# Layer 1 attention of a two-layer decoder trunk: scores of both tiles of tokens in one step

## The chip, the cores and the metric

The kernel runs on one core of one Trainium2 chip. The metric is the device time of one execution in microseconds (us); times below are medians of runs of the same program. The engines are named as in the profile: PE is TensorE's matmuls, PEld its weight loads, DVE is VectorE, ACT is ScalarE, POOL is GpSimd, SP the queue that issues the loads.

## What is computed

Two layers of a decoder trunk on 256 tokens of width 1024, all in float32. Layer 0 has eight heads of block-sparse attention and eight of dilated windows; layer 1 has 16 heads in four groups with three branches, added with sigmoid gates. Each layer ends with a gated feed-forward block and a gated per-layer embedding. The part of layer 1 that the change touches, cut down:

```python
q, kc, vc, ks, vs, kw, vw, g = jnp.split(xn @ w_in, ...)
kc = _rms(_compress(_heads(kc, NSA_GROUPS), *cmp_k), kn_c)     # 15 compressed keys
vc = _compress(_heads(vc, NSA_GROUPS), *cmp_v)
gates = jax.nn.sigmoid(g)                                      # per token, head, branch
s = einsum('bghsd,bgcd->bghsc', qg, kc) * ATTN_SCALE + bias    # branch 1: compressed
o_cmp = softmax(s) @ vc
# branch 2: selected blocks (with 256 tokens: all of them, causal)
# branch 3: sliding window of 512 (with 256 tokens: all, causal)
o = gates[..., 0:1] * o_cmp + gates[..., 1:2] * o_slc + gates[..., 2:3] * o_win
return o.transpose(0, 2, 1, 3).reshape(B, S, D_MODEL) @ w_out
```

## The kernel before

Activations stay on chip, with the features on the partitions. Weights come in units of up to 512 KB: SP loads a unit into one of six `raw` buffers, ACT makes its rounded high part (`hi`), DVE (in layer 1 also POOL, for half of every second unit) the low part (`lo`), and the main matmuls use both. In layer 1 the main matmuls are, in order, the projection chunks (`ic`), the projection of the per-layer embedding (`pa`), the output projection (`oc`), then the feed-forward block (`ga`, `ua`, `da`).

PSUM has eight banks: four for the main accumulators (tag `acc`) and four small ones (tag `st`, `st_tile`, line 76) that all other steps take in turn.

The order of PE and SP is written out by hand. The program keeps an estimated clock `clk`, which every matmul advances by a fixed cost, and a list `side` of generators, each with a due time. After every four to six main matmuls, `tick` (line 169) lets up to six due generators emit a step each; a generator yields the time until it wants to be asked again. `until` (line 174) runs side steps, and nothing else, until a named event has happened by the clock. Where such a step lies in PE's queue is thus fixed when the program is built. ACT, DVE and POOL get their order from the framework.

The side steps of layer 1:

- `compress` (966) makes the 15 compressed keys and values; its last step (`kct`) transposes the keys and sets the event `kc`.
- `split_t`/`q_split` (933) transposes the queries (`qps`).
- `cmp_scores(b)` (1048), once for each half of the heads: scores of the compressed branch (`cs`), a long softmax on DVE and ACT, and, `KN["cmp"]` later, the transposes of its probabilities (`pcp`).
- `attend` (699) drives, for eight heads, the steps of `attn1` (1098). `A(i)` (1102): scores (`s`) of one pair of heads for one tile of 128 tokens, both branches, six matmuls into two small banks; then on DVE four readings with the bias (`neg_scores`, 499), on ACT four exponentials, a reciprocal, and the normalising, on POOL for the first tile and on DVE for the second. The second tile's step also emits a load of the next bias tile on SP (`load_tb1`, 893, called at 1122), into the buffer of a pair whose readings must be over. `B(i)` (1131): two sets of three transposes (`t`) of one head's probabilities into two small banks, copied out by ACT and DVE. `C(k)` (1144): 18 matmuls that give a pair's output (`o`) in one small bank, read by ACT and then DVE (`o_evac`, 495).

`attend` is called with `pb=2, per_a=2, per_s=2` in layer 1: two A steps make a pair, at most two heads may be open when a pair begins, the gap between A steps is `gap1` = 2.4, and B is due `LB1` = 7.66 after the pair's last score step. Layer 0 calls it with `per_s` 1 (lines 829 and 835). `out_proj` (536) waits with `until` for the outputs of two pairs before each quarter of `oc`.

Of the kernel before, what the change touches and what calls it, by code (L numbers as in the profile page):

```python
# [11 lines left out]
F32 = mybir.dt.float32  # L12
# [20 lines left out]


OUT = (1024, 256)
KN = {'stQ': 3.5, 'stF': 7.12, 'stP': 6.0, 'st0': 1.48, 'st1': 11.0, 'sq': 3, 'LSb': 2, 'warm': 4, 'spF': 6.77, 'spP': 5.23, 'burst': 6, 'prep0': 2.6, 'prep1': 2.0, 'qk': 11.39, 'qk2': 12.0, 'qk3': 9.53, 'qk4': 10.0, 'ev': 0.63, 'gap0': 1.54, 'gap1': 2.4, 'LB0': 7.35, 'LB1': 7.66, 'LC': 2.13, 'hT': 5.0, 'cmp': 10.0, 'ev1': 1.0, 'ev2': 1.8, 'c0': 4.0, 'c00': 0.5, 'c1': 4.5, 'c2': 9.0, 'ns': 'PPVV', 'lop': 2, 'ptd': 1, 'pb': 1}


@with_exitstack
def trunk(ctx: ExitStack, tc: tile.TileContext, a, out):  # L40
# [5 lines left out]
    ps = ctx.enter_context(tc.tile_pool(name="ps", bufs=1, space=PS))  # L46
# [26 lines left out]
    def acc_tile(n):  # L73
        return ps.tile([128, 512], F32, tag="acc", name=n, bufs=4)

    def st_tile(n):
        return ps.tile([128, 512], F32, tag="st", name=n, bufs=4)

    def wk_tile(n, shape=(128, 512)):
# [42 lines left out]
    def emit_split():  # L122
# [8 lines left out]
        m = N if i < 3 else n  # L131
        if KN["lop"] and i in l1_units and i % KN["lop"] == 0:
            m = n // 2
        for x in range(0, n, m):
            nc.scalar.activation(hi[:, x:x + m], r[:, x:x + m], AF.Copy)  # L135
            e = nc.gpsimd if KN["lop"] and x and i in l1_units and i % KN["lop"] == 0 else nc.vector
            e.tensor_tensor(lo[:, x:x + m], r[:, x:x + m], hi[:, x:x + m].bitcast(F32), op=OP.subtract)  # L137
# [8 lines left out]
    clk = [0.0]  # L146
    ev = {}
# [11 lines left out]
    def side_step():  # L159
        for e in side:  # L160
            if e[1] <= clk[0]:
                try:
                    e[1] = clk[0] + next(e[0])
                except StopIteration:
                    side.remove(e)
                return True
        return False

    def tick():
        for _ in range(KN["burst"]):  # L170
            if not side_step():
                return
# [24 lines left out]
    def happened(name):  # L197
        return name in ev and ev[name] <= clk[0]

    def take(name, n):  # L200
# [3 lines left out]
        while ws["ld"] < min(i + n + LD, len(units)):  # L204
            emit_load()
        while ws["sp"] < min(i + n + (LS if n == 1 else KN["LSb"]), len(units)):
            emit_split()
# [148 lines left out]
    warm = wk_tile("warm")  # L356
# [8 lines left out]

    keep_busy(KN["warm"])
    nc.scalar.activation(rhb[:, 0:2], ones, AF.Tanh)
# [34 lines left out]
    st = {}  # L402
# [15 lines left out]
    def squares(i):  # L418
# [4 lines left out]
        else:  # L423
            j = wk_tile("sqj")
            nc.scalar.activation(j, two(h, i), AF.Square)  # L425
            e = nc.gpsimd if i < KN["sq"] else nc.vector
            e.tensor_tensor(st["sum"], st["sum"], j, op=OP.add)  # L427
# [271 lines left out]
    def attend(n, A, B, C, gap, lb, p0, ready=(), pb=3, ptb=4, per_pt=1, per_a=1, per_s=1):  # L699

        tA, tB, k, steps, tS = [], [], 0, 0, 0.0
        while 2 * k < n:
            now = clk[0]
            if len(tB) >= 2 * k + 2 and now >= tB[2 * k + 1] + KN["LC"] and all(happened(n) for n in ready):
                C(k)
                ev[f"o{p0 + k}"] = clk[0] + 0.8
                k += 1
                yield 0.0
            elif len(tB) < len(tA) and now >= tA[len(tB)] + lb and (len(tB) - 2 * k) // per_pt < ptb:
                B(len(tB))  # L710
                tB.append(clk[0])
                if len(tB) == n - 2:
                    ev[f"b{p0}"] = clk[0]
                yield 0.0
            elif len(tA) < n and (steps % 2 or len(tA) - len(tB) <= (pb - 1) * per_a) and now >= tS:
                A(steps)
                steps += 1
                tS = clk[0] + gap
                if per_s == 1 or steps % 2 == 0:
                    tS = clk[0] + gap * per_a / per_s  # L720
                    tA += [clk[0] + 0.5 * KN["gap0"] * i for i in range(per_a)]
                yield 0.0
            else:
                yield 0.15
# [241 lines left out]
    def compress(idr):  # L966
# [57 lines left out]
        kc = cmc  # L1024
# [18 lines left out]
        new_x(1)  # L1043
        cmp_homes(0)
        vc_blocks(0)
        ev["kc"] = clk[0] + 0.8

    def cmp_scores(b):
        if b:
# [48 lines left out]
    def attn1(h0):  # L1098
# [44 lines left out]

        def C(k):
            pts = [stt.pop(("pt", 2 * k + e)) for e in range(2)]
            o = ps.tile([128, 512], F32, tag="st", name="o", bufs=4)
            j, gs = k, (h0 // 4, h0 // 4 + 1)
            b = h0 // 8
            for l in range(2):
                mm(o[:, 0:256], VCR[b][:, l, 128 * (j % 2):128 * (j % 2) + 128], PCR[b][:, j // 2], start=l == 0, stop=False)  # L1150
            for br in range(2):
                for t, (x0, x1) in enumerate(((0, 256), (256, 384))):
                    for e in range(2):
                        mm(o[64 * e:64 * e + 64, 128 * t:256], VV[:, t, br, gs[e] * 64:(gs[e] + 1) * 64],
                                         pts[e][:, br, x0:x1], start=False, stop=br == 1 and t == 1)
            o_evac(o, 1, h0 // 2 + k)
# [105 lines left out]
```

## Time and profile before

| what | value |
|---|---|
| median of 3 runs | 706.35 us (705.91 to 706.37) |
| the profiled execution | 707.13 us, of which its span 705.3 us |
| PE busy | 689.8 us (98%) |
| DVE busy | 511.0 us (72%) |
| ACT busy | 413.1 us (59%) |
| POOL busy | 177.6 us (25%) |
| HBM traffic | 171 GB/s over the span |

The span reaches from the first to the last instruction of the profiled execution; its whole time has some 1.8 us around it. In the profile, a busy time of PE contains the modelled ends of matmuls that overlap the next ones, so the start of one matmul to the start of the next is the safer measure of what it cost. A row's bracket tells how long the engine was idle before it, and what ended that. The attention of layer 1 lies between 396 and 487 us.

### The profile page before, as it was taken

How to read it: one execution, taken by the hardware profiler on the slowest of the kernel's cores; microseconds unless marked ns; L12 is line 12 of the kernel's file. 1: busy time of each engine (PE TensorE's matmuls, PEld its weight loads, DVE VectorE, ACT ScalarE, POOL GpSimd, SP SyncE). 2: the span in 40 equal slices, each digit the busy share in tenths (PEclk: the TensorE clock that was granted, in tenths of full speed). 3: DMA queues.
4: the chain of work that ended last, by engine and by line, in shares of the span. 5: the costliest groups of instructions: out<-in, count | busy, mean ns of one | idle time of the engine just before them, and what ended most of it. 6: DMA issues, size and time to landing. Idle time of an engine off the chain costs nothing.

```text
span 705.3 us, 12005 instructions
## 1 busy us (share of the span) xinstructions
PE 689.8 (98%) x4378; PEld 598.0 (85%) x4378; DVE 511.0 (72%) x985; ACT 413.1 (59%) x770; POOL 177.6 (25%) x287
## 2 busy tenths in 40 slices
PE   8999999999999999999999989999999999999997
PEld 6887788998888888889878868878988888888897
DVE  6769775878867774657977788776697778757466
ACT  7547785655655653544664787776465656545343
POOL 1254100133132230001163625341232321310010
PEclk9999999999999999999999999999999999999999
DMA  8955433456566465556773355523557565654611
GB/s 305 328 181 197 164 119 120 139 183 208 165 202 200 163 225 187 183 176 194 213 238 113 118 140 126 155 61 91 153 185 228 163 198 169 218 187 170 213 60 60
DMA packets 69947, 121.66 MB, mean 172 GB/s; under 512 B 5504, under 2 KB 17664, under 8 KB 69888
## 3 DMA queue, kind: packets, MB, share of 16 engines
q1 hardware_dynamic: 69888, 120.89, 53.9%
q8 instruction: 34, 0.56, 0.3%
q14 instruction: 25, 0.20, 0.1%
HBM read 119.83 MB, written 1.05 MB: 171 GB/s over the span
## 4 chain that ended last, share of the span: by engine, by line
PE 80%; DVE 6%; ACT 4%; POOL 3%; issue 3%; DMA 3%; SPq 0%; DVEq 0%; ACTq 0%; POOLq 0%
PE ua L153 18%; PE da L153 17%; PE ga L153 17%; PE oc L153 6%; PE pc L153 5%; PE ic L153 5%; DVE lo L137 3%; PE o L153 3%; PE t L157 2%; PE s L153 2%; PE q L153 2%; PE pa L153 1%; PE v L153 1%; ACT hi L135 1%; DMA raw<-in_w_in_ab_dram 1%
## 5 line engine op out<-in xcount | busy, mean ns | idle before, releaser
L137 DVE TENSOR_TENSOR lo<-raw,hi 128x1024 fp32r<-128x1024 f32 (+2 forms) x218 | 264.2, 1224 | 104.5 <-ACT hi L135 104.4
L135 ACT ACTIVATE hi<-raw 128x1024 fp32r<-128x1024 f32 (+4 forms) x231 | 223.7, 987 | 156.5 <-PE da L153 50.7
L153 PE MATMUL ua<-x,hi 128*128 128x512 f32 (+1 forms) x384 | 96.1, 375 | 0.0
L153 PE MATMUL ga<-x,hi 128*128 128x512 f32 x352 | 92.8, 394 | 1.4 <-DVE h L521 0.9
L153 PE MATMUL da<-big,hi 128*128 128x512 f32 x352 | 89.6, 393 | 0.0
L153 PE MATMUL ic<-hi,x 128*128 128x512 f32 (+2 forms) x256 | 78.5, 376 | 0.2 <-DVE qn L924 0.2
L153 PEld LDWEIGHTS ua<-x,hi 128*128 128x128 f32 x384 | 65.9, 189 | 8.7
L153 PEld LDWEIGHTS da<-big,hi 128*128 128x128 f32 x352 | 62.7, 189 | 10.7
L153 PEld LDWEIGHTS ga<-x,hi 128*128 128x128 f32 x352 | 61.6, 189 | 11.4 <-DVE h L521 1.2
L427 POOL TENSOR_TENSOR sum<-sum,sqj 128x512 f32<-128x512 f32 x12 | 16.9, 1409 | 174.8 <-ACT sqj L425 174.7
L604 POOL TENSOR_TENSOR th<-th,rfb 128x512 f32<-128x512 f32 x22 | 28.5, 1297 | 125.1 <-DVE th L603 118.7
L153 PE MATMUL ua<-x,lo 128*128 128x256 f32 x352 | 57.6, 282 | 0.0
L153 PEld LDWEIGHTS ua<-x,lo 128*128 128x128 f32 x352 | 52.9, 190 | 5.2
L153 PEld LDWEIGHTS ga<-x,lo 128*128 128x128 f32 x352 | 51.3, 189 | 5.6
L153 PEld LDWEIGHTS ic<-hi,x 128*128 128x128 f32 x256 | 46.6, 188 | 10.3 <-issue 2.1
L153 PE MATMUL ga<-x,lo 128*128 128x256 f32 x352 | 52.8, 281 | 0.0
L153 PEld LDWEIGHTS da<-big,lo 128*128 128x128 f32 x352 | 49.1, 190 | 4.2
L153 PE MATMUL da<-big,lo 128*128 128x256 f32 x352 | 50.3, 282 | 0.0
L153 PE MATMUL oc<-x,hi 128*128 128x256 f32 x256 | 48.5, 289 | 0.1
L153 PE MATMUL ic<-lo,x 128*128 128x512 f32 (+2 forms) x128 | 46.9, 366 | 0.0
L153 PE MATMUL pc<-x,hi 128*128 128x256 f32 x256 | 46.6, 284 | 0.0
L613 POOL TENSOR_TENSOR th<-us,th 128x512 f32<-128x512 f32 x20 | 36.4, 1819 | 37.6 <-DVE us L571 37.6
(206 smaller groups left out, 1136.8 us busy)
## 6 DMA issues: line engine op xcount, KB each, us to landing
raw<-in_w_ffn_gate_dram SPq DMA_DIRECT2D x44, 512.0 KB, 3.8
raw<-in_w_ffn_up_dram SPq DMA_DIRECT2D x44, 512.0 KB, 4.4
raw<-in_w_ffn_down_dram SPq DMA_DIRECT2D x44, 512.0 KB, 4.0
raw<-in_w_in_ab_dram SPq DMA_DIRECT2D x23, 512.0 KB, 6.6
raw<-in_w_ple_gate_dram SPq DMA_DIRECT2D x16, 512.0 KB, 3.9
raw<-in_w_in_nsa_dram SPq DMA_DIRECT2D x12, 512.0 KB, 4.6
raw<-in_w_out_ab_dram SPq DMA_DIRECT2D x8, 512.0 KB, 3.3
raw<-in_w_in_nsa_dram SPq DMA_DIRECT2D x16, 256.0 KB, 4.4
```

Source lines behind the costliest of these rows:

```text
L135: nc.scalar.activation(hi[:, x:x + m], r[:, x:x + m], AF.Copy)
L137: e.tensor_tensor(lo[:, x:x + m], r[:, x:x + m], hi[:, x:x + m].bitcast(F32), op=OP.subtract)
L153: nc.tensor.matmul(o, l, r, start=start, stop=stop)
L157: nc.tensor.transpose(o, i, ident if idn is None else idn)
L427: e.tensor_tensor(st["sum"], st["sum"], j, op=OP.add)
L604: nc.gpsimd.tensor_tensor(v2(th), v2(th), r2(), op=OP.mult)
L613: nc.gpsimd.tensor_tensor(y, x, y, op=OP.mult)
```

## The change

Three things are changed. In `attend`, a layer 1 step emits the scores of both tiles of a pair (`A` twice), and only when the planner's clock is 1.2 us (`mA`) past the last time that a small bank was handed out; for 1.5 us (`mB`) after it neither of the two `attend` generators emits anything, and the next pair is due 2.6 us (`gA`) after it. For layer 0 the limit of open heads is now asked at every step, not at every second one. The event `kc` is set 1.4 instead of 0.8 after the transposes of the compressed keys, and `cmp` is 11.6 instead of 10.0. `C` takes its bank through `st_tile`, so that the clock of the last bank counts it as well.

```diff
-KN = {'stQ': 3.5, ... 'cmp': 10.0, ...}
+KN = {'mA': 1.2, 'gA': 2.6, 'mB': 1.5, 'stQ': 3.5, ... 'cmp': 11.6, ...}
...
+    used, held = [0.0], [0.0]
+
     def st_tile(n):
+        used[0] = clk[0]
         return ps.tile([128, 512], F32, tag="st", name=n, bufs=4)
...
-            if len(tB) >= 2 * k + 2 and now >= tB[2 * k + 1] + KN["LC"] and all(happened(n) for n in ready):
+            if per_s == 2 and now < held[0]:
+                yield held[0] - now
+            elif len(tB) >= 2 * k + 2 and now >= tB[2 * k + 1] + KN["LC"] and all(happened(n) for n in ready):
                 C(k)
...
-            elif len(tA) < n and (steps % 2 or len(tA) - len(tB) <= (pb - 1) * per_a) and now >= tS:
-                A(steps)
-                steps += 1
-                tS = clk[0] + gap
-                if per_s == 1 or steps % 2 == 0:
-                    tS = clk[0] + gap * per_a / per_s
-                    tA += [clk[0] + 0.5 * KN["gap0"] * i for i in range(per_a)]
+            elif len(tA) < n and len(tA) - len(tB) <= (pb - 1) * per_a and now >= tS and (
+                    per_s == 1 or now >= used[0] + KN["mA"]):
+
+                for _ in range(per_s):
+                    A(steps)
+                    steps += 1
+                if per_s == 2:
+                    held[0] = clk[0] + KN["mB"]
+                tS = clk[0] + (KN["gA"] if per_s == 2 else gap * per_a)
+                tA += [clk[0] + 0.5 * KN["gap0"] * i for i in range(per_a)]
                 yield 0.0
...
-        ev["kc"] = clk[0] + 0.8
+        ev["kc"] = clk[0] + 1.4
...
-            o = ps.tile([128, 512], F32, tag="st", name="o", bufs=4)
+            o = st_tile("o")
```

## Rows read from the trace of the kernel before

**Rows 1.** The page, its first part: busy us, share of the span, instructions.

```profile
PE 689.8 (98%) x4378; PEld 598.0 (85%) x4378; DVE 511.0 (72%) x985; ACT 413.1 (59%) x770; POOL 177.6 (25%) x287
```

**Rows 2.** By window: us, busy of PE, PEld, DVE, ACT, POOL, clock, DMA, GB/s.

```profile
396.00:441.80 45.80, 42.83 (x307) 33.79 (x305) 39.39 (x145) 35.09 (x106) 20.24 (x34) 1.00 0.45 115
441.80:487.00 45.20, 44.11 (x361) 36.54 (x360) 30.54 (x125) 31.50 (x100) 14.04 (x18) 1.00 0.36 103
```

**Rows 3.** The chain of waits: start us, us, what; undisturbed side steps.

```profile
404.35 0.90 PE s L153 x6
...
428.40 0.55 PE s L153 x6
...
435.62 1.37 PE t L157 x12
```

**Rows 4.** PE timeline, 399 to 410: start, us, operation, [idle before <- releaser].

```profile
399.97 0.40 PE L153 MATMUL ic<-hi,x 128*128 128x512 f32 x1
400.94 1.93 PE L153 MATMUL cs<-kct,big 128*128 128x64 f32 x16 [0.58 <-DVE kct L1042]
...
408.67 0.50 PE L153 MATMUL ic<-hi,x 128*128 128x512 f32 x1
409.01 0.40 PE L153 MATMUL ic<-lo,x 128*128 128x512 f32 x1
409.24 0.62 PE L153 MATMUL ic<-hi,x 128*128 128x512 f32 x2
```

**Rows 5.** PE timeline around the first transposes of the compressed probabilities.

```profile
413.78 0.39 PE L153 MATMUL ic<-hi,x 128*128 128x512 f32 x1
415.73 0.74 PE L157 MATMUL pcp<-ident,big 128*128 128x128 f32 x4 [1.56 <-ACT big L1086]
416.30 0.82 PE L157 MATMUL t<-ident,p 128*128 128x128 f32 x6
...
418.39 0.62 PE L153 MATMUL s<-big,big 64*128 64x256 f32 x6
```

**Rows 6.** PE timeline: transposes behind scores, scores behind transposes.

```profile
424.57 1.03 PE L157 MATMUL t<-ident,p 128*128 128x128 f32 x6
...
426.73 0.48 PE L153 MATMUL pa<-px,hi 128*128 128x256 f32 x2
...
445.33 0.50 PE L153 MATMUL s<-big,big 64*128 64x512 f32 x1
...
447.36 0.50 PE L153 MATMUL oc<-x,hi 128*128 128x256 f32 x2
```

**Rows 7.** PE timeline, 463 to 469.

```profile
463.78 1.07 PE L157 MATMUL t<-ident,p 128*128 128x128 f32 x6
464.78 1.32 PE L153 MATMUL s<-big,big 64*128 64x512 f32 x6
...
466.87 0.35 PE L153 MATMUL s<-big,big 64*128 64x256 f32 x1
...
468.04 0.50 PE L153 MATMUL o<-x 128*128 128x256 f32 x2
```

**Rows 8.** SP timeline (issue of a bias load), then the chain's load behind it.

```profile
407.91 0.37 SPq L897 DMA_DIRECT2D tb<-in_tb_dram  x1
...
409.10 5.22 DMA raw<-in_w_out_nsa_dram
```

**Rows 9.** DVE by line and shape, 396 to 487: busy us, mean ns | idle before.

```profile
L500 DVE CUSTOM_DVE_ANT_0 p<-s,tb 128x256 f32<-128x256 f32 x20 | 7.5, 415 | 0.5 <-PE s L153 0.4
...
L500 DVE CUSTOM_DVE_ANT_0 p<-s,tb 128x128 f32<-128x128 f32 x20 | 4.8, 280 | 0.3 <-PE s L153 0.3
```

**Rows 10.** The chain of waits around the end of the last C step.

```profile
481.75 1.71 PE o L153 x18
...
483.49 0.40 ACT x L496
...
483.90 0.44 DVE x L497
```

More of the change, by code (lines that the diff above doesn't have):

```diff
@@ L35 @@
 OUT = (1024, 256)
-KN = {'stQ': 3.5, 'stF': 7.12, 'stP': 6.0, 'st0': 1.48, 'st1': 11.0, 'sq': 3, 'LSb': 2, 'warm': 4, 'spF': 6.77, 'spP': 5.23, 'burst': 6, 'prep0': 2.6, 'prep1': 2.0, 'qk': 11.39, 'qk2': 12.0, 'qk3': 9.53, 'qk4': 10.0, 'ev': 0.63, 'gap0': 1.54, 'gap1': 2.4, 'LB0': 7.35, 'LB1': 7.66, 'LC': 2.13, 'hT': 5.0, 'cmp': 10.0, 'ev1': 1.0, 'ev2': 1.8, 'c0': 4.0, 'c00': 0.5, 'c1': 4.5, 'c2': 9.0, 'ns': 'PPVV', 'lop': 2, 'ptd': 1, 'pb': 1}
+KN = {'mA': 1.2, 'gA': 2.6, 'mB': 1.5, 'stQ': 3.5, 'stF': 7.12, 'stP': 6.0, 'st0': 1.48, 'st1': 11.0, 'sq': 3, 'LSb': 2, 'warm': 4, 'spF': 6.77, 'spP': 5.23, 'burst': 6, 'prep0': 2.6, 'prep1': 2.0, 'qk': 11.39, 'qk2': 12.0, 'qk3': 9.53, 'qk4': 10.0, 'ev': 0.63, 'gap0': 1.54, 'gap1': 2.4, 'LB0': 7.35, 'LB1': 7.66, 'LC': 2.13, 'hT': 5.0, 'cmp': 11.6, 'ev1': 1.0, 'ev2': 1.8, 'c0': 4.0, 'c00': 0.5, 'c1': 4.5, 'c2': 9.0, 'ns': 'PPVV', 'lop': 2, 'ptd': 1, 'pb': 1}
 @with_exitstack
```

## The prediction

> **What bounds the kernel now.** I read the page first, then the busy time by stretch, then the chain of waits, and last the TensorE timeline of layer 1's attention. The page says that TensorE is busy for 98% of the span [rows 1]. The stretch in which the changed steps run, 396 to 487 us, holds 42.83 + 44.11 = 86.94 us of TensorE work in 91.00 us, at a granted clock of 1.00, the 2.4 GHz level [rows 2]. So the bare idle time there is 4.06 us, and no change of order can win much more than that plus what hides inside "busy". Something does hide: a TensorE step that is held up in its middle counts as busy until its modelled end. I therefore measure from start to start. The chain gives the undisturbed lengths: scores of the first tile of tokens 0.55 us, of the second 0.90, twelve transposes 1.37 [rows 3]. Against these, six places of the timeline are too long. One row of a main matmul starts 0.24 us before the next one (409.01 to 409.24) [rows 4].
>
> - **cs** (compressed scores) starts 0.97 us after the matmul before it, not 0.24: 0.73 lost, to the compressed keys [rows 4].
> - **pcp** starts 1.95 us after its predecessor: 1.71 lost. The row names the ACT copy of the compressed probabilities [rows 5]. Behind that stands the SP queue: the bias load of pair 0 went out only at 407.91, since it waits for that pair's last score readers, and the weight load behind it took from 409.10 another 5.22 us [rows 8]. ACT, which works in order, sat on the split of those weights.
> - **The transposes behind pcp**: 416.30 to 418.39 is 2.09, 0.72 over [rows 5].
> - **Transposes straight behind scores**: 424.57 to 426.73 is 2.16, 0.79 over. I read this as banks that the scores have just filled [rows 6].
> - **Scores straight behind transposes**: 445.33 to 447.36 is 2.03, 1.13 over [rows 6].
> - **The tail**, 463.78 to 468.04: t, s, t, s take 4.26 where 1.37 + 0.90 + 0.55 = 2.82 would do, 1.44 over [rows 7].
>
> Sum: 0.73 + 1.71 + 0.72 + 0.79 + 1.13 + 1.44 = **6.52 us** of lost TensorE time that a better order could give back.
>
> **The change, part by part.**
>
> *Layer 0.* Its `attend` has `per_s` 1, so the new wait and the hold do not apply. What is new is that the odd steps must obey the limit of outstanding heads too. In the present order each of those steps comes when at most four heads are open, and four are allowed (`pb` 3, two heads a step); the due time comes out alike. No instruction moves: 0.
>
> *The order in layer 1.* I walked the side list through by hand with the planner's own costs. The first pair waits for 1.2 us after `kct`, so it comes one tick of main matmuls later than now, with both tiles, and cs comes straight behind it. Then: one pair; two B steps, a tick, the third pair; a tick, pcp, two B steps, C, and straight behind it the fourth pair. So all four pairs of the first half are scored when the last `ic` chunk ends, where now two and a half are. `q_split` of the second half is pushed at the end of that chunk, hence later in the order, and the fifth pair too; that costs nothing as long as `oc` matmuls stand in front, and they do. In the second half two pairs are scored between `oc` steps. After the fourth `oc` unit comes a run without any main matmul: B, B, pcp, pair, C, B, B, pair, C, B, B. Only then the `oc` matmuls go on.
>
> *Saved 1: the six places.* cs and pcp come later by the two due times (0.6 and 1.6), filled with main matmuls: 0.73 + 1.71. Moreover the pair's bias load goes out sooner: pair 0's second tile is scored about 3 us earlier, so its readers end earlier, and SP's weight loads behind the bias load with them. That is the cover of the pcp gain; without it the 1.71 stays. The next three bias loads are moved likewise, each behind the scores of its own pair. The other four places go as places: transposes no longer stand between the two tiles. All 6.52 are counted as removed, and the new waits are counted below.
>
> *Saved 2: fewer steps.* If the streaming time goes with the columns, the second tile (0.90) has twice the first's (0.55), so 0.35 is streaming and **0.20 us** of each step is fixed [rows 3]. Eight steps go away: 1.60. The main matmul behind a step pays as well: 0.34 to its successor, where 0.24 is usual [rows 4]; eight of these would make 0.8 more. I take 1.60, since several joined steps have no main matmul behind them; ends 0 (the pair pays the fixed part twice all the same) and 2.40.
>
> *Added 1: four banks at once.* The scores of one pair now go into all four `st` banks. A step straight ahead must have been read out, and a step straight behind waits for the first readers. VectorE needs at most 4 x 0.280 + 4 x 0.415 = 2.78 us for the eight readings [rows 9]. A C step's bank is free 0.88 us after its last matmul (481.75 + 1.71 to 483.90 + 0.44) [rows 10]; transposes ahead of scores cost the 1.13 above. The planner's rule asks for 1.2 us since the *start* of the last step, which a C step outlasts by itself, so it protects little there. Place by place:
> - first pair, whose fourth bank is that of `kct`: 0.3.
> - pairs with a tick of main matmuls behind the transposes: 0.3 in all.
> - the fourth pair straight behind C: its last bank is wanted some 0.5 us after C, free after 0.88: 0.4.
> - in the run without main matmuls, the pair behind pcp: 0.8; the pair straight behind four transposed tiles: near the 1.13, 1.0.
> - transposes behind a pcp or a C: 0.3 each, three times.
> - cs or C straight behind a pair: their bank's two readings (2 x 0.28) end while the second tile streams (0.69): 0.
> Sum 0.3 + 0.3 + 0.4 + 0.8 + 1.0 + 0.9 = **3.7 us**. The ends are 0 and the full price of both neighbours at all eight pairs, 8 x (0.79 + 1.13) = 15.4. I stay near the low end since a wait in the planner (`mB`) keeps B and C out for 1.5 us, and main matmuls fill it at five of the eight pairs.
>
> *Softmax latency.* Pair to B stays at 7.66 us in the planner, and by the walk no B step comes sooner behind its pair than 6.5 us. Eight exponentials instead of four arrive at ACT together, but in total nothing is added on VectorE, ACT or GpSimd. Counted at 0; if that cover fails, the first B of the run without main matmuls shows it.
>
> **Sum.** 6.5 + 1.6 - 3.7 = 4.4 us. The profiled execution took 707.13 us, of which 705.3 are its span; it lies 0.78 above the median of 706.35, so the gain is taken off the median: 706.35 - 4.4 = 701.95, **702.0 us**. The stages behind are bound by TensorE and keep their length, so that the gain reaches the end.
>
> **Rivals.**
>
> *Slower: the banks.* One mechanism: with all four banks in one step, TensorE waits at both neighbours of the pair at the price it pays today, 0.79 + 1.13 = 1.92 each time [rows 6]. The point from which it decides is (6.5 + 1.6) / 8 = 1.0 us a pair; above 1.2 the kernel is slower by more than 0.2%. At five of eight pairs it is 9.6 - 8.1 = 1.5 us slower, 707.9; at six 3.4, 709.8. For it: the run without main matmuls, and C straight ahead of a pair. Against it: five pairs have main matmuls on one side at least. The Trainium skill speaks for this rival: "Perfetto Trace Analysis", Optimizing Tensor Performance, says that independent matmul groups should rotate through the banks, so that reading out one overlaps the matmuls of the next; a pair that takes all four leaves nothing to rotate. By that rule the waits of [rows 6] would come at every pair; the trace agrees that they exist, and no run here shows how often they would come.
>
> *About the same: VectorE.* Up to 441.80 it is busy 39.39 of 45.80 us, 86% [rows 2]. The same work in 42 us would be 94%, and banks would come free late. If the first half can't shrink at all, the second half remains: 1.13 + 1.44 recovered, half of the fixed parts (0.8), less its own new waits (0.8 + 1.0 + 0.6): 1.0 us faster, 705.4. For it: that share. Against it: much of VectorE's work there is for weight splits, which follow the main matmuls, not the pairs.
>
> *Only the due times work.* 0.73 + 1.71 = 2.4 stay and the joined steps give back what they cost: 703.9, inside the forecast's own band.
>
> *More.* New waits of 1.5 us or less and the full fixed part: 6.5 + 1.6 - 1.5 = 6.6, 699.7.
>
> **How the numbers follow.** A kernel like this can be told from no change from about 0.2%, 1.4 us, on. Forecast with the due times alone inside its band (700.5 to 704.9): 0.53. More than that: 0.10. VectorE, within 0.2%: 0.19. Slower, the banks: 0.18. The range leaves out half of "more" and most of "slower" beyond 708.3: 699.5 to 708.3. Faster 0.53 + 0.10 = 0.63, same 0.19, slower 0.18.
>
> **What would show it.** Right: no idle before cs and pcp; eight score steps of twelve matmuls, each near 1.25 us; the start of the last `oc` unit, now behind C at some 483.4 [rows 10], near 479; the bias loads on SP at about 403, 410, 418 and 425. Wrong: score steps of 2 us or more, with ACT or VectorE readers of `t` or `o` as releasers; B steps that wait for p; VectorE above 93% of the first half; a wait of the main matmuls for weights. If cs or pcp still waits, the due times missed their cover.

## The result, and the profile after

The changed kernel takes **713.41 us** (median of 4 runs, 713.27 to 714.03); the kernel before, run beside it, 706.13 (4 runs). The ratio is 1.0099, with a 95% interval of 1.0081 to 1.0117. The prediction was 702.0 us, in a range that ended at 708.3: wrong in sign, and outside the range.

The profiled execution has a span of 711.6 us. The first part of its page (busy us, share, instructions):

```profile
PE 693.2 (97%) x4378; PEld 601.7 (85%) x4378; DVE 510.9 (72%) x985; ACT 412.8 (58%) x770; POOL 178.5 (25%) x287
```

The counts are those of [rows 1]: the same instructions in another order. By window, with the columns of [rows 2], the attention as a whole and then two stretches of it:

```profile
396.00:441.80 45.80, 42.29 (x295) 33.62 (x294) 35.94 (x136) 34.35 (x107) 20.47 (x34) 0.96 0.48 119
441.80:487.00 45.20, 41.08 (x320) 33.46 (x319) 30.88 (x128) 29.46 (x96) 13.19 (x18) 0.92 0.27 83
403.00:406.80 3.80, 3.80 (x11) 2.93 (x11) 3.13 (x13) 1.96 (x5) 2.17 (x4) 0.55 0.78 206
464.50:471.60 7.10, 6.91 (x33) 4.25 (x33) 4.35 (x26) 5.11 (x22) 3.72 (x7) 0.52 0.07 25
```

The joined step, the twelve score matmuls of two tiles, is called a pair below. Two things stand here. TensorE did fewer matmuls in the same windows (295 + 320, before 307 + 361). And the granted clock, 1.00 all along in [rows 2], fell to about half, the 1.2 GHz level, in two places. The waits of TensorE from 396 to 487 (total, times, longest), the first four:

```profile
PE pcp L160 <- DVE nm L503: 2.8, 2, 1.5
PE t L160 <- DVE big L1137: 1.2, 1, 1.2
PE s L156 <- DVE x L500: 1.0, 1, 1.0
PE t L160 <- DVE nm L503: 0.8, 1, 0.8
```

All four releasers are VectorE; the waits left out are 0.4 us and less, two of them on ACT. `nm` is the last part of a reading of scores, `big` at 1137 is the normalising, `x` at 500 the reading of `o`; the lines correspond to 500, 1129 and 497 of before.

**Where the time went.** From the start of the `kct` transposes to the first `ga` matmul the profiled executions take 92.72 us before and 99.44 after, 6.72 us more; the two spans differ by 6.3 (711.6 and 705.3), so the whole difference lies here. Summed from the start of each TensorE instruction to the start of the next, by the step it belongs to:

| step | before | after | difference |
|---|---|---|---|
| scores `s`, 96 matmuls | 13.71 | 17.53 | +3.82 |
| transposes `t`, 96 | 12.95 | 15.43 | +2.48 |
| outputs `o`, 144 | 14.51 | 16.20 | +1.69 |
| main `ic`, 54 | 15.31 | 14.57 | -0.74 |
| `cs`, `pcp`, `qps` | 5.50 | 5.07 | -0.43 |
| main `pa`, `oc`, and `kct` | 30.74 | 30.63 | -0.11 |

A wait ahead of a step is in the row of the step before it. So the waits of cs and pcp in [rows 4, 5] are in `ic` of before, and the new waits of pcp are in `s` of after.

The TensorE timeline of after in the first half (start, us, operation, [idle before <- releaser]):

```profile
399.08 1.92 PE L156 MATMUL s<-big,big 64*128 64x256 f32 x12
400.93 1.96 PE L156 MATMUL cs<-kct,big 128*128 128x64 f32 x16
402.74 0.48 PE L156 MATMUL ic<-hi,x 128*128 128x512 f32 x1
...
407.26 1.32 PE L156 MATMUL s<-big,big 64*128 64x256 f32 x12
408.50 0.50 PE L156 MATMUL ic<-hi,x 128*128 128x512 f32 x1
...
415.51 1.32 PE L156 MATMUL s<-big,big 64*128 64x256 f32 x12
418.32 0.63 PE L160 MATMUL pcp<-ident,big 128*128 128x128 f32 x4 [1.49 <-DVE nm L503]
```

The pair at 407.26 gives way to a main matmul 1.24 us later: this is the joined step as forecast. cs follows its pair without idle time. But twelve rows of `ic` behind cs take 4.52 us (402.74 to 407.26), where the same twelve take 2.94 undisturbed: the clock. And pcp, which the change moves out of a wait, waits again, for the readings of the pair straight ahead of it: 2.81 us from the start of that pair to pcp. VectorE at that place:

```profile
414.00 1.58 DVE L1093 TENSOR_TENSOR big<-csw,x 128x120 f32<-128x120 f32 x2
415.50 0.60 DVE L1137 TENSOR_SCALAR p<-p,rl 128x256 f32<-128x256 f32 x2
416.02 0.60 DVE L1137 TENSOR_SCALAR big<-big,rl 128x256 f32<-128x256 f32 x2
416.55 1.21 DVE L140 TENSOR_TENSOR lo<-raw,hi 128x1024 fp32r<-128x1024 f32 x1
417.69 0.28 DVE L503 CUSTOM_DVE_ANT_0 big<-s,tb 128x128 f32<-128x128 f32 x1
```

VectorE comes to the first reading at 417.69, 2.18 us after the pair began: the normalising of an earlier pair and a weight split stand ahead of it in the queue. The two operations ahead of these took 1.58 us, where the same two take 0.47 at 459.12; GpSimd was at work beside them (last section). In the second half, the run without main matmuls:

```profile
457.57 1.32 PE L156 MATMUL s<-big,big 64*128 64x256 f32 x12
460.23 0.63 PE L160 MATMUL pcp<-ident,big 128*128 128x128 f32 x4 [1.33 <-DVE nm L503]
...
462.18 0.77 PE L160 MATMUL t<-ident,big 128*128 128x128 f32 x5 [1.22 <-DVE big L1137]
463.75 0.52 PE L160 MATMUL t<-ident,big 128*128 128x128 f32 x3 [0.80 <-DVE nm L503]
464.44 0.58 PE L160 MATMUL t<-ident,big 128*128 128x128 f32 x3 [0.17 <-DVE rl L1133]
464.95 1.51 PE L156 MATMUL s<-big,big 64*128 64x256 f32 x7
466.65 1.62 PE L156 MATMUL s<-big,big 64*128 64x512 f32 x5 [0.19 <-DVE nm L503]
468.20 0.80 PE L156 MATMUL o<-x 128*128 128x256 f32 x2
468.92 2.81 PE L156 MATMUL o<-pt,big 128*64 128x256 f32 x16
```

TensorE was idle for 3.5 us between 458.8 and 464.5; then come scores and `o` at half clock, the sixteen matmuls of `o` with 2.81 us where 1.52 is usual. VectorE and GpSimd in the same run:

```profile
457.83 1.27 DVE L140 TENSOR_TENSOR lo<-raw,hi 128x1024 fp32r<-128x1024 f32 x1 [0.93 <-ACT hi L138]
...
459.51 0.28 DVE L503 CUSTOM_DVE_ANT_0 p<-s,tb 128x128 f32<-128x128 f32 x1
...
460.43 1.44 DVE L140 TENSOR_TENSOR lo<-raw,hi 128x512 fp32r<-128x512 f32 x1
461.79 1.13 DVE L1137 TENSOR_SCALAR big<-big,rl 128x256 f32<-128x256 f32 x4
462.84 0.41 DVE L503 CUSTOM_DVE_ANT_0 p<-s,tb 128x256 f32<-128x256 f32 x1
```

```profile
460.05 1.26 POOL L140 TENSOR_TENSOR lo<-raw,hi 128x512 fp32r<-128x512 f32 x1
```

The pair scored at 451.81 is normalised at 461.79 to 462.92, up to 9.9 us after the end of its scores (453.06); the B step behind it waited for just that. Two weight splits, and the first four readings of the next pair, stood ahead of it. Not all of that was VectorE's queue: on ACT the pair's last exponential stood behind a weight split too (456.76, 1.04 us) and began only at 457.71.

### The profile page after: what moved, and what is told of

Its sections match the earlier page's. It is cut to its first block, busy times and chain, and to the rows that moved or that the text cites. A ratio compares the mean times of both kernels' runs of the same rounds, so it can differ in the third digit from the quotient of the medians.

```text
span 711.6 us, 12002 instructions
## 1 busy us (share of the span) xinstructions
PE 693.2 (97%) x4378; PEld 601.7 (85%) x4378; DVE 510.9 (72%) x985; ACT 412.8 (58%) x770; POOL 178.5 (25%) x287
## 3 DMA queue, kind: packets, MB, share of 16 engines
HBM read 119.83 MB, written 1.05 MB: 170 GB/s over the span
## 4 chain that ended last, share of the span: by engine, by line
PE 81%; DVE 8%; ACT 4%; POOL 3%; issue 3%; DMA 2%; SPq 0%; ACTq 0%; DVEq 0%; POOLq 0%
PE ua L156 17%; PE da L156 17%; PE ga L156 17%; PE ic L156 6%; PE oc L156 5%; PE pc L156 4%; DVE lo L140 3%; PE o L156 3%; PE t L160 2%; PE v L156 2%; PE s L156 2%; PE q L156 2%; PE pa L156 1%; ACT hi L138 1%; DMA raw<-in_w_in_nsa_dram 1%
```

## The experiments

Ratios are against the kernel before, run on the same chip beside it, with 95% intervals; "0.2%" is the bound of the prediction. The first theory from these two traces was: the walk put pcp and cs in the wrong places, and the rest is the clock. The rivals were the due times, the joined step itself, the SP queue and VectorE's queue.

### Due times and places

**due_only**: the kernel before with the two due times.

```diff
-KN = {... 'cmp': 10.0, ...}
+KN = {... 'cmp': 11.6, ...}
-        ev["kc"] = clk[0] + 0.8
+        ev["kc"] = clk[0] + 1.4
```

> The kernel before with the two due times of the change alone (kc 1.4, cmp 11.6); scores as before, one tile of tokens in a step. Theory (the loss comes from the joined score steps, through waits and two falls of the granted clock): this kernel recovers the waits before cs and pcp, 0.73 + 1.71 = 2.4 us, and loses nothing: about 703.9, clock 1.00 all through. Rival (the due times do the harm, since pcp then falls behind scores): 708 or more.

Measured: 709.43 us (10 runs), 1.0034 [1.0022, 1.0046]. Slower by 0.3% instead of faster by 2.4 us. pcp still waits, and now behind transposes:

```profile
416.23 0.52 PE L157 MATMUL t<-ident,p 128*128 128x128 f32 x3 [0.77 <-DVE nm L500]
417.71 0.64 PE L157 MATMUL pcp<-ident,big 128*128 128x128 f32 x4 [0.97 <-DVE pt L1139]
```

Behind them the granted clock is 0.53 from 418.0 to 425.2. Moving a step by time does not move the work it waits for; it changes what stands ahead of it.

**due_undone**: the changed kernel with the two old due times (the same two lines turned round).

> The changed kernel with the two due times set back (kc 0.8, cmp 10.0); scores joined. Theory: the joined steps carry the loss. The first pcp no longer stands behind the third pair, which saves its 1.5 us, the run without main matmuls in the second half stays as it is, with its waits and its half clock (some 3.5 us): 711 to 713. Rival (the due times do the harm): back to about 706.

Measured: 712.69 us, 1.0080 [1.0053, 1.0108]. So most of the loss needs no due time. The first pcp's wait is gone, and waits of 1.57, 1.38 and 0.87 us stand ahead of scores instead, the middle one on ACT.

**cs_apart**: the first cs one tick later, pcp where it was.

```diff
-        yield KN["cmp"]
+        yield KN["cmp"] - (0 if b else 1.28)
...
-wait(KN["ev1"]), cmp_scores(0)
+wait(KN["ev1"] + 1.0), cmp_scores(0)
```

> The changed kernel; the first cs step comes one tick of main matmuls (six of 512 columns) later, everything else in the same place. Theory (the first fall of the clock, 403.3 to 406.7, comes from the scores of a pair with cs straight behind, 3.7 us of small matmuls): no fall there, the twelve ic matmuls behind take 2.9 instead of 4.5 us, total 711.5 to 712. Rival (the clock falls there whatever stands around): unchanged, 713.4.

Measured: 713.33 us, 1.0090 [1.0065, 1.0116]. The fall of the clock at 403 is gone. But the next pair waits 1.0 us for the reading of cs (`csw`), and the fall in the second half is longer, from 462.2 to 472.5, where the changed kernel's goes from 464.8 to 471.6. So what the first fall costs by itself is not shown by this run.

**pcp_apart**: the changed kernel with `cmp` 12.6, so that pcp stands a tick behind the pair, the order that the prediction priced.

> The changed kernel with cmp 12.6 in place of 11.6: the first pcp comes one tick behind the third pair, with B, B, C and the fourth pair behind it, which is the order that the prediction was worked out for; in the second half two B steps stand ahead of pcp. If the prediction only had the order wrong, and its prices right: 702 to 704. Theory (the prices were wrong too: in the run without main matmuls the B steps wait for the softmax and the clock falls): the 1.5 us before the first pcp go, the second half stays: 710 to 712.

Measured: 716.27 us, 1.0131 [1.0106, 1.0156], slower still. pcp waits 0.2 us, but the C step behind it finds the compressed probabilities not yet copied by ACT:

```profile
423.24 0.51 PE L156 MATMUL o<-x 128*128 128x256 f32 x2 [2.76 <-ACT x L1103]
```

So the prices failed, not only the places.

### The clock, the bias load, earlier queries

**fill_tail**: the changed kernel with 18 matmuls more, of 512 columns, that add zeros to an accumulator in use: six ahead of the second pcp, and six ahead of each of the two B steps behind it.

```diff
+    def idle_fill(n):
+        for _ in range(n):
+            nc.tensor.matmul(live["acc"], zero[0], px[:, 0].rearrange("p e s -> p (e s)"), start=False, stop=False)
...
         yield KN["cmp"]
+        if b:
+            idle_fill(6)
         p = st_tile("pcp")
...
         def B(i):
+            if h0 and i < 2:
+                idle_fill(6)
```

> The changed kernel with 18 added matmuls of 512 columns that add zero times data to an output accumulator: six ahead of the second pcp, six ahead of each of the two B steps behind it, where TensorE waits today (1.33 + 1.22 + 0.80 us idle). They are 3.8 us of added work. Theory (the second fall of the clock, 464.8 to 471.6, follows from that idle stretch and costs 3.5 us): the waits are filled, the clock stays at 1.00 there, and the kernel gets faster although it does more: 710 to 711. Rival (the fall comes anyway, or the waits alone cost the time): 713.4 or up to 3.8 us more.

Measured: 711.37 us, 1.0058 [1.0041, 1.0076], with more work than the changed kernel at 1.0099. The clock stays at 1.00, in the second half:

```profile
441.80:487.00 45.20, 43.56 (x354) 36.05 (x353) 32.14 (x129) 29.45 (x96) 13.47 (x18) 1.00 0.25 74
```

and the pair and `o` behind the fill run at full speed:

```profile
465.12 1.66 PE L156 MATMUL s<-big,big 64*128 64x256 f32 x12
466.71 0.51 PE L156 MATMUL o<-x 128*128 128x256 f32 x2
467.14 1.52 PE L156 MATMUL o<-pt,big 128*64 128x256 f32 x16
468.60 1.81 PE L160 MATMUL t<-ident,p 128*128 128x128 f32 x12
```

Scores 1.59 and `o` 1.89 us from start to start, against 3.25 and 3.47 of after: 3.2 us of clock. Part of the better median has another source: in the profiled run the fall at 403 is missing too, where nothing was changed.

**early2**: `qk4` 5.0 instead of 10.0 in the changed kernel, so that the queries of the second half come earlier.

> The changed kernel with qk4 5.0 in place of 10.0: the queries of the second half, and with them its compressed scores and pairs, come some 2.5 us earlier in the order; the run without main matmuls stays, but the softmax of its first pair is further ahead of its B steps. Theory (waits for p and a fall of the clock in that run): about 1.2 us of the wait for p go, the fall may stay: 710.5 to 712.5. Rival (only the adjacency of steps and banks counts): 713.4.

Measured: 714.27 us, 1.0093 [1.0078, 1.0108]: no gain.

**tb_late**: the kernel before, with the bias load issued in every second B step rather than in the second tile's A step.

```diff
-            if t and len(TB) < 8:
-                load_tb1()
...
         def B(i):
+            if i % 2 == 0 and len(TB) < 8:
+                load_tb1()
```

> The kernel before with the bias loads of the second half issued in the B steps in place of the second tile's scores; no order of TensorE changes. If the reading of the wait before pcp holds (SP held by the bias load until 407.9, weights late, ACT held), the 1.7 us before pcp and most of the 0.7 behind it go: about 704.2. Rival (ACT is late there for other reasons): 706.4.

Measured: 705.91 us (10 runs), 0.9984 [0.9974, 0.9995]. pcp's wait is gone. From the matmul before it to pcp it is 0.23 us (415.43 to 415.66) instead of 1.95. This execution alone does not yet show that the reading of [rows 5, 8] was right: in it (707.06 us, mean clock 0.996) the clock falls behind cs, and TensorE comes to the place 1.65 us later than before (415.43 against 413.78), which would cover the wait by itself. tb_fill below shows it at full clock. The net gain is smaller than 1.7; the five runs at 0.998 or more took 704.98 to 705.65. The fall:

```profile
402.80:406.40 3.60, 3.60 (x12) 2.47 (x13) 2.09 (x7) 0.66 (x1) 2.02 (x4) 0.53 0.41 88
```

**kc_only**: the kernel before with only the event `kc` moved to 1.4.

> The kernel before with the event kc 0.6 later and nothing else; the first cs then comes a tick later, its pcp behind it, and the order of the second half shifts. Theory (the wait before cs is 0.7 us, but every order that piles pcp, B and scores up pays for it): between 705.6 and 708. Rival (the move of cmp alone did the harm in the kernel with both due times): 705.6 or less.

Measured: 709.52 us (10 runs), 1.0029 [1.0017, 1.0041]. The wait of cs, 0.73 us, is gone, and pcp's grows to 2.47 (on ACT `sq`), with the clock at half behind it (418.5 to 425.3). This one moved due time makes the loss of due_only by itself.

### The joined step

**split_pair**: the changed kernel, but the second tile's A step comes one tick (0.6 us of the planner's clock) behind the first's.

```diff
-                for _ in range(per_s):
-                    A(steps)
-                    steps += 1
+                A(steps)
+                steps += 1
                 if per_s == 2:
-                    held[0] = clk[0] + KN["mB"]
+                    tS = clk[0] + 0.6
+                    held[0] = tS
+                    yield 0.0
+                    continue
```

and a branch ahead of it that emits the second tile when `tS` has come.

> The changed kernel, but the second tile of a pair is scored one tick of main matmuls behind the first, as its own step with two banks; due times, gap (gA), hold (mB) and the limit at the start of a pair as changed. Theory (the joined step is what makes neighbours wait, 11.4 us of waits in all, and the clock falls after such waits): most of the loss goes, 706 to 709. Rival (the later order as such, with the run without main matmuls, does it): 712 or more.

Measured: 713.32 us, 1.0090 [1.0072, 1.0109]. Seven of the eight pairs are scored apart here (the eighth, at 471.79, has no main matmul between its tiles), and the loss is the same: the joined step is not needed for it, and my theory that four banks at once make the waits fell. Scores never wait here (idle 0.0 ahead of all 96), but the transposes do, and pcp most:

```profile
418.68 0.74 PE L160 MATMUL pcp<-ident,big 128*128 128x128 f32 x4 [3.11 <-ACT big L1106]
```

**joined_first** and **joined_second**: the new `attend` for one half of the heads only, the old one (with both due times new) for the other.

> The changed kernel, but the heads of the second half follow the old rule (one tile in a step, gap 2.4). By the trace of the changed kernel the first half is 2 us behind the kernel before when the embedding's projection ends, and the rest is lost in the second half. Theory (waits and falls follow joined steps): 708.5 to 710. Rival (the second half suffers since it starts later, whatever its steps): 712 or more.

> The changed kernel, but the heads of the first half follow the old rule; the due times stay moved. The kernel before with these due times alone took 709.4. Theory (losses of the joined steps in the second half add to that): 712 to 714. Rival (joined steps in the second half cost nothing by themselves): 709.4.

Measured: 713.74 us, 1.0090 [1.0071, 1.0109], and 713.89, 1.0094 [1.0075, 1.0112]. Each half alone makes the whole loss; they don't add up. In both, as in the changed kernel, the clock falls in each half (at 402.7 and 464.2; at 420.7 and 454.8).

**tb_fill**: tb_late with three zero matmuls ahead of the first cs, where the kernel before is idle for 0.58 us.

```diff
+        if b == 0:
+            idle_fill(3)
         pv = st_tile("cs").rearrange("p (t j e l c) -> p t j e l c", t=2, j=4, e=2, l=2)
```

> The kernel before with the bias loads issued in the B steps, which took away the wait before pcp but showed a fall of the clock behind the first cs in its profile (402.9 to 406.4), and three added matmuls that add zero, straight ahead of that cs, where TensorE waits 0.57 us. Theory (a fall follows a stretch of waits and small matmuls): the clock stays, 704.5 to 705.3. Rival (the added work costs its 0.65 us and the clock does as before): 706.5.

Measured: **704.86 us** (7 runs, 704.45 to 705.56), 0.9968 [0.9958, 0.9979]: faster than both kernels, with the clock at 1.00 in both windows. TensorE comes to pcp at nearly the time of the kernel before (413.94 against 413.78) and does not wait; pcp starts 1.56 us earlier. So the bias load was behind that wait, as [rows 5, 8] were read:

```profile
413.94 0.39 PE L153 MATMUL ic<-hi,x 128*128 128x512 f32 x1
414.17 0.60 PE L157 MATMUL pcp<-ident,big 128*128 128x128 f32 x4
```

### SP, both falls, and VectorE

**after_tb**: the changed kernel with tb_late's edit.

> The changed kernel with the bias loads of the second half issued in the B steps, as in tb_late. Theory (the lost time of the changed order comes from the softmax queued on ACT and VectorE and from the clock, in the second half above all, where no bias load is issued): 712 to 713.5. Rival (SP, held by the bias loads, delays weights and splits, and these delay the readers of the banks): 709 or less.

Measured: 712.77 us, 1.0084 [1.0055, 1.0112]. In the new order the SP queue is not what is late.

**due_tb**: due_only with tb_late's edit.

> The kernel before with the two moved due times and the bias loads in the B steps. The due times alone took 709.4. Theory (those 3 us are mostly the first half's 3.4 us of waits at the first B steps and pcp and the fall of the clock behind them, and there the readers are held by splits that wait for weights behind the bias load): 705 to 706.5. Rival (the first B steps wait for banks of scores whatever SP does): 709.

Measured: 707.70 us (10 runs), 1.0009 [0.9998, 1.0021]: a quarter of a per cent below due_only, and still not faster than before.

**fill_both**: fill_tail and the three matmuls ahead of the first cs.

> The kernel fill_tail with three more added matmuls of zeros ahead of the first cs. Theory: clock 1.00 in every run, 711.5 to 712 (0.65 us more work than fill_tail, no first fall); what is then left above the kernel before, some 5 us with about 4.4 us of added matmuls in it, is waits alone. Rival (the falls come at random): clocks below 1.00 as often as in the changed kernel.

Measured: 711.55 us, 1.0071 [1.0048, 1.0094]. Three of four runs have a mean clock of 0.999 or 1.000 and are no faster than 711.5, against 706.59 of before: with the clock held, some 5 us of waits and filling remain. The remaining run, the profiled one (0.996), shows a fall from 417.4 to 420.9, where the changed kernel has none, so filling these two places did not keep the clock in every run.

**no_norm**: the changed kernel without the normalising of the two masked branches (VectorE for the second tile, GpSimd for the first); the output is another.

```diff
-            for x, _, _, c in parts:
-                (nc.vector if t else nc.gpsimd).tensor_scalar(x, x, r[:, c:c + 1], None, op0=OP.mult)
```

> The changed kernel without the normalising of the probabilities of layer 1's two masked branches (left out on GpSimd and VectorE, so these branches are not divided by their sums). No step of TensorE changes. Theory (the first B steps in the run without main matmuls wait for the softmax, whose last link is this normalising behind a weight split on VectorE): idle time of t there falls from 2.2 us to under 1, total 709.5 to 712. Rival (they wait for banks, as at other places): 713.4.

Measured: 706.26 us (10 runs), 0.9988 [0.9973, 1.0003]. The whole loss against the kernel before is gone, which is more than the theory expected. pcp in the first half, which waited 1.49 us straight behind its pair, doesn't wait, and VectorE comes to the first reading 0.65 us after the pair began, not 2.18 (the pair itself still takes 1.88 us from start to start). TensorE and then VectorE:

```profile
414.11 1.95 PE L156 MATMUL s<-big,big 64*128 64x256 f32 x12
415.99 0.66 PE L160 MATMUL pcp<-ident,big 128*128 128x128 f32 x4
```

```profile
414.76 0.29 DVE L503 CUSTOM_DVE_ANT_0 big<-s,tb 128x128 f32<-128x128 f32 x1
```

In the run without main matmuls the theory was not borne out: the idle time of the transposes falls from 2.19 us to 1.31, not below 1, and its releaser is now a reading of scores. In its profiled execution the clock stays at 1.00 in the whole attention.

**before_no_norm**: the same lines taken out of the kernel before, the control.

> The kernel before without the normalising of the two masked branches' probabilities (left out on GpSimd and VectorE, as in no_norm): the control of no_norm. No step of TensorE changes. Theory (in the old order the normalising is covered, in the changed one it isn't): 704 to 706, little below the kernel before, so that most of the 7 us between the two orders go with the normalising. Rival (the normalising costs either order the same): about 699, 7 us below.

Measured: 707.85 us (10 runs), 1.0005 [0.9994, 1.0016]. In the old order that work costs nothing: it lies beside TensorE's.

**no_norm_dve**: the changed kernel without VectorE's share of the normalising only.

```diff
-            for x, _, _, c in parts:
-                (nc.vector if t else nc.gpsimd).tensor_scalar(x, x, r[:, c:c + 1], None, op0=OP.mult)
+            for x, _, _, c in parts if not t else []:
+                nc.gpsimd.tensor_scalar(x, x, r[:, c:c + 1], None, op0=OP.mult)
```

> The changed kernel without the normalising of the second tiles on VectorE (4 x 8 instructions, 10.5 us of VectorE in the stretch); GpSimd still normalises the first tiles. Theory (VectorE's own time, with bank readings and splits queued behind it, makes TensorE wait): nearly all of no_norm's gain, 706 to 708. Rival (GpSimd's normalising is the late link, or slows VectorE): 711 or more.

Measured: 707.67 us (10 runs), 1.0004 [0.9994, 1.0014]. Nearly the whole gain of no_norm is VectorE's. Here too pcp in the first half (415.46) doesn't wait. What VectorE was rid of, from the groups by line and shape of the changed kernel (busy us, mean ns | idle before), is 9.6 us of work:

```profile
L1137 DVE TENSOR_SCALAR p<-p,rl 128x256 f32<-128x256 f32 x20 | 6.0, 354 | 0.1
L1137 DVE TENSOR_SCALAR big<-big,rl 128x256 f32<-128x256 f32 x12 | 3.6, 345 | 0.0
```

The clock still falls once in its profiled run (0.50 from 458.4 to 465.2).

## Why the prediction was wrong

**What held.** The lost places were real: in tb_fill the waits of cs and pcp are gone and the time is lower, and in the changed kernel cs has no idle time ahead of it. The cause of pcp's wait (SP's bias load, then ACT) was read rightly, and tb_fill shows it. The saved fixed part of a step was right: an undisturbed pair takes 1.24 and 1.25 us (at 407.26 and 451.81), where 0.55 + 0.90 = 1.45 was paid [rows 3]. The bias loads went out sooner, at 402.33 and 410.25 as forecast and at 420.01 and 429.89 where 418 and 425 were named. No main matmul waited for weights.

**The term that failed: "Added 1", 3.7 us.** With undisturbed lengths of 1.25 for a pair, 1.37 for twelve transposes, 1.78 for `o`, and 12.50 for the 54 rows of `ic` (their sum in no_norm), the table above leaves 17.53 - 10.00 = 7.53, 15.43 - 10.96 = 4.47, 16.20 - 14.24 = 1.96 and 14.57 - 12.50 = 2.07: 16.0 us over. Some 4.9 of it is the clock (below), so the waits are 11.1 and not 3.7. Five of the eight pairs took 1.85 to 3.25 us from their start to the start of the step behind them instead of 1.25, a sixth 1.76 (1.66 of the 3.25 is the clock). cs straight behind a pair, priced at 0, cost 0.60 of it (1.85 - 1.25). The ends of the range, 0 and 15.4, held the true value; I took a value near the low end because the hold `mB` and main matmuls were to lie between. They did not cover it, because what freed a bank was not the time since the pair but VectorE's arrival at its readings. The 2.78 us of eight readings were priced from their own durations [rows 9], as if VectorE stood ready; at 415.51 it came 2.18 us late, behind 1.05 us of normalising and a weight split of 1.14 us. So too with the bank of a C step, priced as free 0.88 us after it [rows 10]: the first C ends at 422.63, and VectorE reads it 4.45 us later, behind a split of 1.73 us and the normalising. The pair of 425.73 waits for that in its middle and takes 2.71 us to the step behind it, 1.46 over, where 0.4 was added:

```profile
424.29 1.73 DVE L140 TENSOR_TENSOR lo<-raw,hi 128x512 fp32r<-128x512 f32 x1
427.08 0.41 DVE L500 TENSOR_TENSOR x<-o,x 128x256 fp32r<-128x256 f32 x1
427.55 0.96 PE L156 MATMUL s<-big,big 64*128 64x512 f32 x5 [0.97 <-DVE x L500]
```

The normalising is not all of this term. By the same sum no_norm, at full clock, is still 7.7 us over (4.73 for the scores, 2.68 for the transposes, 0.31 for the outputs). So 3.4 of the 11.1 go with the normalising and, with them, the falls of the clock; that is enough to lose nothing, but 4.0 more than the 3.7 stay, and 6.5 + 1.6 - 7.7 = 0.4 is no gain worth the name. So no_norm ends near the kernel before and not near 702.

**"Softmax latency: 0"** failed in the same place. I argued that nothing is added on VectorE in total. True, and beside the point: the next pair's first four readings, two weight splits and the rest of the compressed softmax stood ahead of a normalising, which was over 9.9 us after its scores, against 7.66 in the planner. I had named the sign (the first B of the run without main matmuls waits for its p), and there it is: 1.22 us at 462.18. Its net price was less: without the normalising the transposes there still wait 1.31 us, for readings of scores, where their waits were 2.19 in all.

**The two due times, 2.4 us of "Saved 1",** failed: alone they cost 0.3%. cs lost its wait, but pcp left one and met another, with a fall of the clock behind it. The cover that I named, main matmuls, was there; the bank and ACT's queue were not looked at.

**A step of the walk.** A generator's new due time is `e[1] = clk[0] + next(e[0])`, and the clock is read before the step is emitted. I counted it from the step's end. So pcp stands straight behind the third pair, and straight behind a pair in the second half, and not a tick later. But pcp_apart, in the order I priced, is slower still, so this mistake doesn't explain the sign.

**A term that was missing: the clock.** The sum had no price for it, since [rows 2] show 1.00. At half clock the twelve `ic` rows cost 4.52 - 2.94 = 1.58 more, and in the second half `o` 3.47 - 1.78 = 1.69 and the pair 3.25 - 1.59 = 1.66: 4.9 us. fill_tail shows the second half of this directly.

**The rivals.** "Slower: the banks" was the right direction, with its point of decision right too (1.0 us a pair; 11.1 / 8 = 1.4 came). Its times, 707.9 to 709.8, lacked the clock. "About the same: VectorE" was right in its engine and wrong in its form: I tied it to a share of 93% in the first half, and the share fell, from 86% to 35.94 / 45.80 = 78%, while VectorE became the releaser of nearly every wait. What counted was what stood ahead of one instruction in the queue, not the share. no_norm, no_norm_dve and the control together show that: the same normalising cost nothing in the old order (1.0005 without it) and 1.1% in the new one (1.0099 with it, 0.9988 without), 1.0 of it by VectorE's part. They take away two things at once, the work ahead of other readings and the last link before a B step; the pcp of the first half shows the first, the 1.22 us at 462.18 the second, and their shares of the whole are not shown. The Trainium skill's rule that I put beside the first rival ("Perfetto Trace Analysis", Optimizing Tensor Performance: rotate through the banks) agrees with the waits of pcp for `nm`, but split_pair, which leaves the banks to rotate between the tiles, is as slow.

**In sum**: a gain of 4.4 was forecast and a loss of 6.7 came in the trace. Of the 11.1 between them 11.1 - 3.7 = 7.4 are waits, 4.9 the clock; the rest, -1.2, is 0.5 that the small steps of the table gave back and 0.7 that the old order lost beyond the six places.

**Left open.** What the 4.0 us of waits are that stay in no_norm. How much of VectorE's lateness is GpSimd's doing (last section). Why joined_first and joined_second each cost as much as both together: what is shown is only that every one of these orders has waits on VectorE and a fall of the clock in both halves. And why the fall at 403 comes in some orders and executions and not in others (below). Which of the remaining waits of no_norm's run without main matmuls (1.27 ahead of pcp, 1.31 ahead of transposes) could be had by a better order was not tried.

## What to carry to other kernels

Before a step is moved or joined, list what stands ahead of its readers in their engine's queue at that place, and price the wait from there, not from the readers' own durations and not from the engine's share of the span. Put main matmuls in the midst of steps of small matmuls that wait for each other, not only ahead of the run: here the run without any paid twice, in waits and then in clock. Taking the suspected engine's work away in both orders, the new and the old, is a cheap test of whether that work delays anything at all.

## What the runs showed of the hardware

**The granted clock falls inside a kernel that is 97% busy.** In the changed kernel it fell to the 1.2 GHz level at 403.3, where TensorE had just run a pair and cs for 3.66 us with 0.13 us of idle time, small matmuls of 64 to 512 columns; and at 464.8, behind 7.2 us of a pair, pcp and transposes with 3.5 us of waits. In tb_late it fell behind an idle 0.57 us and a cs; with three zero matmuls in that place (tb_fill) it stayed at 1.00, and so it did in the second half of fill_tail with its eighteen. It isn't settled by the order alone: fill_tail and no_norm have the same pair and cs (3.64 and 3.65 us) and no fall behind them; the kernel before has the same 0.58 and cs and no fall in its profiled execution, while other runs of it have a mean clock of 0.996 to 0.998; on one chip five runs of it at 0.996 took 707.0 to 708.0 us and four at 1.000 took 706.4 to 706.7. The mean clock does not order the times by itself: ten runs at 0.998 on the same chip took 705.5 to 708.4.

**VectorE takes longer beside GpSimd.** The split of 128 x 512 at 460.43 took 1.44 us on VectorE, where 0.69 is what the same shape took at 451.08, while GpSimd's split ran to 461.31; the split of 424.29 above took 1.73 beside GpSimd's of 424.18 (1.29 us), the two operations of 414.00 1.58 instead of 0.47 beside that of 413.95 (1.29 us); and a tiny operation beside another of GpSimd's took 1.27, where it takes 0.16 at 405.76:

```profile
451.08 0.69 DVE L140 TENSOR_TENSOR lo<-raw,hi 128x512 fp32r<-128x512 f32 x1
451.69 1.27 DVE L1080 TENSOR_SCALAR cm<-cm 128x16 f32<-128x16 f32 x1
```

```profile
451.64 1.28 POOL L140 TENSOR_TENSOR lo<-raw,hi 128x512 fp32r<-128x512 f32 x1 [12.41 <-ACT hi L138]
```

These last two end together, at 451.64 + 1.28 = 452.92 and 451.69 + 1.27 = 452.96; the two splits of VectorE end some 0.55 us after GpSimd's. The Trainium skill has the rule for it ("SBUF — State Buffer", Who interferes with whom): one pair of ports is shared by the two engines under an exclusive lock, so that the one that comes second waits; of VectorE's operations this holds for those with two inputs in SBUF, as the splits have, and for some with one. The trace agrees: in all four places GpSimd's operation began first. Two of them lie just ahead of late readings (417.69 and 427.08), where VectorE lost some 1.1 and 1.0 us, so this is a rival for part of the waits. No run here takes GpSimd's half of the splits away, so what it costs the kernel is not shown; in no_norm_dve it is still there (1.27 us at 412.49) and pcp's wait in the first half is gone.
